# Output projection of a hybrid mixer layer: pairs of token tiles with seven block products in place of eight, conv weights split during the scan

## The chip, the cores and the metric

The kernel runs on one core of a Trainium2 chip. The metric is the device time of one execution in microseconds, as the median of several runs. One execution was also recorded by the hardware profiler; all times of single instructions come from that one. The engines are called as the profile calls them: PE (matmul), DVE (VectorE), ACT (ScalarE), POOL (GpSimd), SP (the queue from which most DMAs are issued); "PEld" is the weight load of a matmul.

## What is computed

One layer with 2176 tokens (128 of context, 2048 latent) and 1024 channels. The reference, cut to what matters:

```python
h = _rmsnorm(x, norm_g) * (1.0 + scale) + shift
proj = h @ w_in                                   # 1024 -> 4096
r, k, v, g_a, b_gate, c_gate, u_conv, g_b = split(proj)
ya, s_final = _wkv(h, token_shift(r, k, v))       # bidirectional delta-rule scan, 8 heads x 64
ya = ya * silu(g_a)                               # 512 channels ("attention half")
yb = b_gate * short_conv(c_gate * u_conv) * silu(g_b)   # 512 channels ("conv half")
u = concatenate([ya, yb], axis=-1) @ w_out        # 1024 x 1024
y = rmsnorm(x + gate * u, final_g)
```

The last two lines are what the change is about: for each of 17 tiles of 128 tokens, [ya, yb] (128 x 1024) times w_out (1024 x 1024), then a gate per channel, the residual, and a normalisation.

## The kernel before

There are three phases in one program, and a scheduler that places the instructions of each engine ahead of time: it walks the program in the order in which it is written, estimates when each instruction could run, and fixes one order for each engine from that. On the chip every engine works through its own fixed list and waits, at each instruction, for the semaphores of what it needs. So an instruction whose data come late holds up everything behind it on its engine. Only PE's list is tied to the written order during the scan, by `behind` (L834), which chains each matmul to the one ahead of it.

*Phase 1* (up to about 1006 us) makes the projections with w_in, the token shifts and the conv half yb, which is complete here and is stored to a DRAM scratch `mixT` (channels x tokens).

*Phase 2* (about 1006 to 1451 us) is the scan. It has 17 stages of two blocks; the loop over `s` in `main` (L1255) plays a string of tokens, `ROUND` (L750), for each: `S` and `b`, `B`, `L`, `u`, `U` each advance a generator of small matmuls (64 to 128 wide) and their copies, `f` and `T` finish an earlier block and store its rows of ya to `mixT`. In each round ACT copies psum to SBUF for the next step (fg<-psX, fg<-psG, E<-psE, zr, zb; L830 and L832), DVE masks and subtracts (L1042, L1049, L1110, L1148), and POOL solves the blocks' triangular systems (L948, L951), one after the other until 1322 us. Psum has eight banks: three for the states (`O.pS`), three for the small products (`O.p2`), and two more (`O.pm`) that the scan uses until stage 14 of 17 and then gives up (`O.pm.close()`).

*Phase 3* is the output projection. Float32 operands are split in a high part (fp32r) and the remainder, and a product x w is made as three matmuls, hi hi + hi lo + lo hi (`products`, L1385, L1389 to L1391). A tile of tokens is the stationary operand, four blocks of 128 channels for the conv half (CONV, rows 512 to 1023 of w_out) and four for the attention half (ATT); a matmul moves 128 x 512 of the weights. Each tile so has 2 column halves x 8 channel blocks x 3 = 48 matmuls. `weights` and `ahead` (L1395, L1401) start in the last three rounds of the scan: they load and split the four conv blocks of w_out on POOL and make the conv halves of two tiles (5 and 6), in tiles of psum called psa. `tail` (L1418) splits the attention blocks of the weights, and then, for each tile in the order TILES: loads of the mixed rows (`load_m`, L1373; mxc and mxa, cast by ACT at L1381, remainder by DVE at L1382), the residual rows (L1440), 48 matmuls in psu (24 where the conv half was made ahead), the gate product from psum on DVE (L1452; L1454 for tiles made ahead), the residual addition on POOL (L1456), squares on ACT (L1457), the scale (L1458 to L1460), the normalisation on DVE (L1462) and the store (L1463).

## Time and profile before

| | |
|---|---|
| median of 3 runs | 1641.16 us (1639.65 to 1644.22) |
| the profiled execution | 1645.99 us |
| its span, first to last instruction | 1644.2 us |
| mean granted TensorE clock | 0.976 |
| PE busy | 1517.7 us, 17160 matmuls |
| POOL busy | 589.2 us |

The profiled execution lies 4.8 us above the median, and 1.8 us of it lie outside the span. A row of a group gives the line, engine, operation, output and inputs, shapes and count; then the busy time, the mean of one instruction in ns, and the idle time of the engine ahead of these instructions with what ended most of it. A row of the timeline gives start and duration, the DMA queue or engine, line and operation, a count where rows alike were put together, and in brackets the idle time before. A row of a DMA group ends with the size of one transfer and the median time from issue to landing.

### The profile page before, as it was taken

The numbers are of one execution on the slowest core, as the hardware profiler recorded it, in microseconds if no ns is written. First come the engines' busy times: TensorE is split into PE (matmuls) and PEld (weight loads), VectorE is DVE, ScalarE is ACT, GpSimd is POOL, SyncE is SP. The second block draws the span as 40 slices with busy tenths as digits, with TensorE's granted clock in tenths as the row PEclk, the third lists the DMA queues.
The fourth block names the chain that finished last, engine by engine and source line by source line (L and its number), as shares of the span: only waits on it lengthen the run. The fifth ranks groups of instructions, "written<-read, shape, count | busy, mean of one in ns | idle before, by whom it ended". The sixth has DMA issues, their size and how long they took to land.

```text
span 1644.2 us, 42415 instructions
## 1 busy us (share of the span) xinstructions
PE 1517.7 (92%) x17160; PEld 1389.9 (85%) x17160; DVE 1100.5 (67%) x2220; ACT 764.5 (46%) x1617; POOL 589.2 (36%) x1040
## 2 busy tenths in 40 slices
PE   5899999999999999999999898988888888689998
PEld 2889998999999999999988898878777777568886
DVE  5886978784738685657788784576776764574333
ACT  4544565554425452425554023767675664432222
POOL 0011211110102021102667363888888851022221
PEclk7999999999999999999999999999999999989999
DMA  9677768664746564655867857867666754254342
GB/s 378 209 264 251 242 233 284 211 228 181 236 156 195 177 208 151 204 181 194 280 202 226 284 174 219 220 190 195 191 190 164 201 136 114 63 199 162 126 151 93
DMA packets 237988, 327.23 MB, mean 199 GB/s; under 512 B 91288, under 2 KB 191896, under 8 KB 223712
## 3 DMA queue, kind: packets, MB, share of 16 engines
q1 hardware_dynamic: 231840, 318.55, 60.8%
q0 software_dynamic: 1200, 3.93, 0.6%
q8 instruction: 135, 2.21, 0.6%
q10 hardware_dynamic: 4752, 2.04, 0.6%
q14 instruction: 61, 0.50, 0.1%
HBM read 207.92 MB, written 116.54 MB: 197 GB/s over the span
## 4 chain that ended last, share of the span: by engine, by line
PE 45%; DVE 9%; POOL 7%; ACT 5%; DMA 4%; issue 3%; SPq 0%; DVEq 0%; ACTq 0%; POOLq 0%
PE psu L1389 4%; PE psu L1390 4%; PE psu L1391 4%; PE psE L841 3%; POOL zt L951 3%; ACT fg L830 2%; POOL ztmp L948 2%; PE psS L841 2%; PE mmc L166 1%; PE mmg L168 1%; PE mmg L166 1%; PE mmg L167 1%; PE mmc L167 1%; PE mmc L168 1%; PE mmv L166 1%
## 5 line engine op out<-in xcount | busy, mean ns | idle before, releaser
L951 POOL TENSOR_TENSOR zt<-zt,ztmp 128x30 f32<-128x30 f32 (+7 forms) x390 | 153.3, 393 | 30.6
L841 PE MATMUL psE<-fg 128*64 128x128 f32 x2176 | 146.4, 277 | 3.4 <-ACT fg L830 1.8
L841 PE MATMUL psS<-sv,E 128*64 128x64 f32 x2176 | 99.4, 231 | 33.2 <-DVE sv L1148 28.5
L841 PEld LDWEIGHTS psE<-fg 128*64 128x64 f32 x2176 | 120.4, 140 | 5.0 <-ACT fg L830 2.2
L841 PEld LDWEIGHTS psS<-sv,E 128*64 128x64 f32 x2176 | 81.2, 141 | 50.7 <-DVE sv L1148 38.3
L329 POOL TENSOR_TENSOR shk<-rawl 128x384 f32<-128x384 f32 (+1 forms) x24 | 25.3, 1052 | 243.1 <-ACT rawl L325 223.8
L1049 DVE TENSOR_TENSOR fg<-psG,consts 64x256 f32<-64x256 f32 x136 | 57.4, 422 | 72.7 <-PE psG L841 35.7
L832 ACT COPY E<-psE 128x256 f32<-128x256 f32 x136 | 50.3, 372 | 107.6 <-DVE E L1110 98.5
L830 ACT ACTIVATE fg<-psX 64x512 f32<-64x512 f32 x136 | 80.4, 591 | 26.7 <-PE psX L841 24.3
L1456 POOL TENSOR_TENSOR z<-z,x 128x512 f32<-128x512 f32 x32 | 41.8, 1307 | 137.5 <-DVE z L1452 114.0
L948 POOL TENSOR_TENSOR ztmp<-ab,zt 128x60 f32<-128x60 f32 (+4 forms) x165 | 86.2, 523 | 12.9
L1110 DVE TENSOR_TENSOR E<-psE,consts 128x256 f32<-128x256 f32 x136 | 56.4, 416 | 39.1 <-PE psE L841 37.1
L329 POOL TENSOR_TENSOR shv<-rawl 128x384 f32<-128x384 f32 (+1 forms) x24 | 20.9, 870 | 166.4 <-ACT rawl L325 164.9
L1148 DVE TENSOR_TENSOR sv<-psS,pc 64x128 f32<-64x128 f32 x254 | 64.8, 277 | 22.9 <-PE psS L841 20.7
L446 POOL COPY pcs<-pp 128x6 f32<-128x6 f32 (+1 forms) x48 | 20.9, 437 | 137.8 <-ACT pp L435 133.9
L166 PE MATMUL mmc<-h,w 128*128 128x384 f32 (+1 forms) x192 | 64.7, 337 | 5.9 <-ACT q1r L327 4.1
L166 PE MATMUL mmg<-h,w 128*128 128x384 f32 (+1 forms) x192 | 64.2, 334 | 3.8 <-ACT q1v L327 3.8
L832 ACT COPY fg<-psG 64x256 f32<-64x256 f32 x136 | 49.8, 366 | 32.8 <-DMA fg<-scr_ops 17.1
L166 PE MATMUL mmb<-h,w 128*128 128x384 f32 (+1 forms) x192 | 62.9, 328 | 1.5 <-ACT ta L439 1.5
L166 PE MATMUL mmgb<-h,w 128*128 128x384 f32 (+1 forms) x192 | 64.0, 333 | 0.3 <-ACT q1r L327 0.3
L167 PE MATMUL mmg<-h,w 128*128 128x384 f32 (+1 forms) x192 | 63.9, 333 | 0.0
L166 PE MATMUL mmv<-h,w 128*128 128x384 f32 (+1 forms) x192 | 63.6, 332 | 0.2 <-ACT q1r L327 0.2
(325 smaller groups left out, 5131.3 us busy)
## 6 DMA issues: line engine op xcount, KB each, us to landing
w<-scr_wsp SPq DMA_DIRECT2D x68, 1024.0 KB, 6.6
scr_wsp<-w SPq DMA_DIRECT2D x34, 1024.0 KB, 4.9
scr_ops<-pair SPq DMA_DIRECT2D x80, 384.0 KB, 3.9
wr<-in_win SPq DMA_DIRECT2D x34, 512.0 KB, 6.3
o<-scr_ops SPq DMA_DIRECT2D x32, 512.0 KB, 4.7
fg<-scr_ops SPq DMA_DIRECT2D x120, 128.0 KB, 4.3
x<-in_x SPq DMA_DIRECT2D x17, 512.0 KB, 3.7
wadas<-in_wada SPq DMA_DIRECT2D x8, 1024.0 KB
```

The source lines that it names most:

```text
L166: T.matmul(ps[:, :n], w[:, 0, k], hh[:, 0, k, :n], start=k == 0, stop=False)
L167: T.matmul(ps[:, :n], w[:, 0, k], hh[:, 1, k, :n], start=False, stop=False)
L830: P.activation(dst, src, AF.Copy, scale=-1.0)
L832: P.copy(dst, src)
L841: r = T.matmul(*a, start=True, stop=True, **k)
L948: eng.tensor_tensor(tv, ab[:, j:j + 2, j + 2:32].unsqueeze(1).broadcast_to((128, kn, 2, n)), zt[:, :kn, j:j + 2].unsqueeze(3).broadcast_to ...
L951: last = eng.tensor_tensor(zt[:, :kn, j + 2:32], zt[:, :kn, j + 2:32], tv[:, :, r], ALU.subtract).ins
L1049: V.tensor_tensor(g.gs[H[1 - h], g.op, h, us], ps[gi][r, :, 64:128], B.mG[r, g.d].unsqueeze(1).broadcast_to((64, 4, 64)), ALU.mult)
L1148: r = V.tensor_tensor(dst, sp[gi][0:64, q], B.pc[0:64, d, 2 * p:2 * p + 2, c:c + 1].broadcast_to((64, 2, 64)), ALU.mult)
L1389: T.matmul(ps[:], mh[:, n], hi[:, cs], start=start and n == 0, stop=False)
L1390: T.matmul(ps[:], mh[:, n], lo[:, cs], start=False, stop=False)
L1391: T.matmul(ps[:], ml[:, n], hi[:, cs], start=False, stop=stop and n == 3)
```

## The change

It has three parts.

*Pairs.* Fourteen of the 17 tiles are taken two at a time (PAIRS). With tile i on top of tile j, and the conv and attention halves of the rows as the two block columns, the product with w_out is a 2 x 2 block product. In place of eight block products (each 4 channel blocks x 3 = 12 matmuls), the pair makes seven, P1 to P7, of sums: S1 = A21 + A22, S2 = S1 - A11, S3 = A11 - A21, S4 = A12 - S2 of the rows (A11 and A12 are tile i's conv and attention rows, A21 and A22 tile j's), made by POOL for each pair, and four sums of weight blocks ("forms" 0 to 3), made once. Seven additions on DVE put the products together. Each input of a product is split in hi and lo by ACT and DVE as before.

*The sums of the weights* are made in the last rounds of the scan by POOL (`sums`, four blocks of work), split, stored to a DRAM scratch `tw`, and loaded again: form 1 by `first_form` at stage 15, form 2 over the second halves of the conv weights, forms 0 and 3 in `rest`, after the scan's pools have closed.

*Earlier work.* The conv weights are split during rounds 1 to 8 (`conv_weights`, one half block of 128 x 512 per round; a raw tile with one buffer, the cast on ACT, the subtraction on DVE). Three tiles (5, 6 and 0) have their conv halves made ahead, in the scan's own banks (`fill`, token `A`), so that `O.pm` stays open to the scan's end; these matmuls are chained into PE's list (`pin`). One copy of states (`held`) goes from POOL to DVE. The rest moves tiles to places in SBUF that are free by then.

The diff, cut to its core:

```diff
-ROUND_END = "f L b L u U S b S b U S b b S L B L T S B S B S B S B B".split()
-ROUND_LAST = "S b S b S b S b".split()
+ROUND_END = "f L b L A u U S b S b U S b b S L B L A A T S B S B S B S B B".split()
+ROUND_FILL = "f L b L A u U S b S b U S b S b L B L A T S B S B S B S B".split()
+ROUND_LAST = "A S b S b S b S b A".split()
...
+        K.weights()
+        O.l1 = Pool(K, "p2l1", "left")
-        O.l1 = Pool(K, "p2l1", "left")
...
+    def pin(r):
+        behind(r, O.last)
+        O.last = r.ins
...
-                    G.tensor_copy(sv[0:64, u], held.pop(gi)[:])
+                    V.tensor_copy(sv[0:64, u], held.pop(gi)[:])
...
+            if 1 <= s <= 8:
+                next(conv)
+            if s == NST - 4:
+                fill = K.fill()
+                next(fill)
+                sums = K.sums()
+                next(sums)
+                next(sums)
             if s == NST - 3:
-                O.pm.close()
-                O.pm = None
-                K.weights()
-                tail = K.ahead()
+                K.early_att()
+                next(sums)
+                next(sums)
+            if s == NST - 2:
+                K.first_form()
...
-                run(tail)
+                run(fill)
+                O.pm.close()
+                O.pm = None
...
-    TILES = [5, 6, 7, 8, 9, 10, 11, 12, 0, 13, 14, 15, 16, 1, 2, 3, 4]
-    AHEAD = TILES[:2]
-    z0 = {}
-    def load_raw(k):
-        raw = O.r.tile([128, 1024], F32, tag="raw", name=f"woraw{k}", bufs=2)
-        D(raw[:], A["wout"][k * 128:(k + 1) * 128, :])
-        return raw
-    def load_k(k, hi, lo, eng, raw=None):
-        copy = P.copy if raw is None else G.tensor_copy
-        raw = raw or load_raw(k)
-        copy(hi[:], raw[:])
-        eng.tensor_tensor(lo[:], raw[:], hi[:].bitcast(F32), ALU.subtract)
-        wk[k] = (hi, lo)
-    def load_m(pool, i, ks, b, copy=P.copy, eng=V):
-        t0 = i * 128
-        a = "c" if ks is CONV else "a"
-        mx = O.r.tile([128, 4, 128], F32, tag="raw", name=f"mx{a}{i}", bufs=2)
-        D(mx[:], S["mixT"].rearrange("(k p) t -> p k t", p=128)[:, ks[0]:ks[0] + 4, t0:t0 + 128])
-        mh = pool.tile([128, 4, 128], F32R, tag=f"mh{a}", name=f"mh{a}{i}", bufs=b)
-        ml = pool.tile([128, 4, 128], F32R, tag=f"ml{a}", name=f"ml{a}{i}", bufs=b)
-        copy(mh[:], mx[:])
-        eng.tensor_tensor(ml[:], mx[:], mh[:].bitcast(F32), ALU.subtract)
-        return mh, ml
-    def products(ps, ms, cs, ks, start, stop):
-        mh, ml = ms
-        for n, k in enumerate(ks):
-            hi, lo = wk[k]
-            T.matmul(ps[:], mh[:, n], hi[:, cs], start=start and n == 0, stop=False)
-            T.matmul(ps[:], mh[:, n], lo[:, cs], start=False, stop=False)
-            T.matmul(ps[:], ml[:, n], hi[:, cs], start=False, stop=stop and n == 3)
+    AHEAD = [5, 6, 0]
+    PAIRS = [(7, 8), (9, 10), (11, 12), (13, 14), (15, 16), (1, 2), (3, 4)]
...
+    def split(hi, lo, raw, copy, eng):
+        copy(hi, raw)
+        eng.tensor_tensor(lo, raw, hi.bitcast(F32), ALU.subtract)
 
     def weights():
         O.r = Pool(K, "p3r", "left")
+    def conv_weights():
+        for k in CONV:
+            hi, lo = wk[k] = [O.r.tile([128, 1024], F32R, name=f"wo{x}{k}") for x in "hl"]
+            for c in HALF:
+                raw = O.r.tile([128, 512], F32, tag="raw", name=f"woraw{k}", bufs=1)
+                D(raw[:], A["wout"][k * 128:(k + 1) * 128, c])
+                split(hi[:, c], lo[:, c], raw[:], P.copy, V)
+                yield
...
+    def product(ps, m, w, start=True, stop=True, pin=lambda r: None):
+        hi, lo = m
+        for n in range(4):
+            wh, wl = w(n)
+            c = slice(n * 128, n * 128 + 128)
+            pin(T.matmul(ps[:], hi[:, c], wh, start=start and n == 0, stop=False))
+            pin(T.matmul(ps[:], hi[:, c], wl, start=False, stop=False))
+            pin(T.matmul(ps[:], lo[:, c], wh, start=False, stop=stop and n == 3))
...
+    def fill():
+        def prepare(i):
+            raw = O.r.tile([128, 512], F32, tag="raw", name=f"mxc{i}", bufs=1)
+            load_mix(raw[:], i, CONV)
+            t = K.spare(f"mhc{i}", F32R, "ab2")
+            m = t[:, 0:512], t[:, 512:1024]
+            split(*m, raw[:], G.tensor_copy, G)
+            return m
+        places = ["a1", "ztmp", "a2", "a3"]
...
+                ps = K.ps_tile([128, 512], f"psa{i}_{h}")
+                product(ps, m, plain(CONV, h), pin=K.pin)
+                if n < 2:
+                    z0[i][h] = K.spare(f"z0_{i}{h}", F32, places.pop(0), 512)[:]
+                P.copy(z0[i][h], ps[:])
+                if h and n < 2:
+                    m = prepare(AHEAD[n + 1])
...
+    def sums():
+        sub = lambda o, x, y: G.tensor_tensor(o, x, y, ALU.subtract)
+        n = 0
+        for k in range(4):
+            t = [K.spare(f"sum{x}{k}", F32, x) for x in ("o10", "o11")]
+            for x, r in zip(t, (k + 4, k)):
+                D(x[:], A["wout"][r * 128:r * 128 + 128, :])
+            (c0, c1), (a0, a1) = [[x[:, h] for h in HALF] for x in t]
+            for f, o, x, y in ((0, c0, c1, c0), (2, c1, a1, c1), (1, a1, a1, c0), (3, a0, a0, a1)):
+                sub(o, x, y)
+            for f, x in ((1, a1), (2, c1), (0, c0), (3, a0)):
+                n += 1
+                if n % 2:
+                    u = K.spare(f"sumh{n}", F32R, "ab")
+                    u = u[:, 0:512], u[:, 512:1024]
+                else:
+                    u = [K.spare(f"sumh{n}{b}", F32R, "zt", 512)[:] for b in range(2)]
+                split(*u, x, G.tensor_copy, G)
+                for b in range(2):
+                    D(S["tw"][f, b, :, k], u[b].bitcast(F32))
+            yield
...
+    def early_att():
+        att_weights(0, K.spare("woraw0", F32, "o10"), G, *[K.spare(f"wo{x}0", F32R, f"o2{n}") for n, x in enumerate("hl")])
...
+            new("A11", (i, CONV))
+            new("A21", (j, CONV))
+            new("A22", (j, ATT))
+            new("A12", (i, ATT))
+            yield f
+            for o, x, y, op in (("S3", "A11", "A21", ALU.subtract), ("S1", "A21", "A22", ALU.add), ("S2", "S1", "A11", ALU.subtract)):
+                new(o)
+                G.tensor_tensor(raw[o], raw[x], raw[y], op)
...
+            zi, zj = [[r.z[:, h] for h in HALF] for r in (ri, rj)]
+            P.copy(zi[0], made("P1", "A11", plain(CONV, 0))[:])
+            nf = next(nxt, None)
+            p2 = made("P2", "A12", plain(ATT, 0))
+            next(nxt, None)
+            p7 = made("P7", "S3", form_b(2))
+            next(nxt, None)
+            p5 = made("P5", "S1", form_b(0))
+            next(nxt, None)
+            p6 = made("P6", "S2", form_b(1))
+            add(zj[1], p6, zi[0])
+            add(zi[0], p2, zi[0])
+            half(ri, 0)
+            add(zj[0], p7, zj[1])
+            add(zi[1], p5, zj[1])
+            add(zj[1], p5, zj[0])
+            half(rj, 1)
+            next(nxt, None)
+            p4 = made("P4", "A22", form_b(3))
+            add(zj[0], p4, zj[0])
+            half(rj, 0)
+            next(nxt, None)
+            p3 = made("P3", "S4", plain(ATT, 1))
+            add(zi[1], p3, zi[1])
+            half(ri, 1)
...
+        for f in (0, 3):
+            t = [O.t.tile([128, 4, 512], F32R, name=f"t{f}{x}") for x in "hl"]
+            for b in range(2):
+                D(t[b][:].bitcast(F32), S["tw"][f, b])
+            form[f] = [[x[:, n] for n in range(4)] for x in t]
```

Line numbers below are those of the kernel that the row is from; in the changed kernel the split of weights and rows is at L1385 and L1386 with its weight loads at L1396, the matmuls at L1429 to L1431, the loads of mixed rows at L1421, the residual rows at L1539 and the loads of forms 0 and 3 at L1667.

**ACT at the scan's start.** In these rows E, fg, zr and zb are the scan's operands, psX, psG, psE and psU its psum tiles, and x2 stands for two rows alike. Before:

```order
L832 COPY E_912_11064<-psE0_1_01_11087 128x4x64
L830 ACTIVATE fg0_9816<-psX0_0_1_11196 64x2x256 x2
L830 ACTIVATE fg1_9817<-psX0_1_1_11197 64x2x256 x2
L1073 ACTIVATE zb_9826<-zc_919_11171,consts_9809 128x16x32 x2
L832 COPY fg0_9816<-psG1_0_0_11218 64x256
L832 COPY fg1_9817<-psG1_1_0_11219 64x256
```

Now (woh4 to woh7 are the high parts of the conv weights, woraw the loaded halves):

```order
L834 COPY E_912_11068<-psE0_1_01_11091 128x4x64
L1385 CAST woh4_11582<-woraw4_11584 128x512
L1385 CAST woh4_11582<-woraw4_12064 128x512
L832 ACTIVATE fg0_9817<-psX0_0_1_11200 64x2x256 x2
L832 ACTIVATE fg1_9818<-psX0_1_1_11201 64x2x256 x2
L1079 ACTIVATE zb_9827<-zc_919_11175,consts_9810 128x16x32 x2
L1385 CAST woh5_12542<-woraw5_12544 128x512
L834 COPY fg0_9817<-psG1_0_0_11222 64x256
L834 COPY fg1_9818<-psG1_1_0_11223 64x256
```

The eight casts of the conv weights, written in rounds 1 to 8, stand among the copies of the first round, the first two ahead of the first fg<-psX.

**SP at the end of the scan and the start of the projection.** Before (gb and fg are gate and gain rows, mxa and mxc a tile's attention and conv rows, x its residual rows, yo the scan's last outputs):

```order
L1424 DMA gb_18922<-scr_gate_68 128x1024 x2
L1426 DMA fg_18925<-in_fg 128x1024
L1440 DMA x35_18945<-in_x 128x1024
L1440 DMA x36_19005<-in_x 128x1024
L1186 DMA sg_1265_19137<-scr_sg_61 128x512
L1378 DMA mxa5_18939<-scr_mixT_63 128x4x128
L1220 DMA scr_mixT_63<-yo_1264_18876 128x4x128
L1378 DMA mxa6_18999<-scr_mixT_63 128x4x128
L1186 DMA w_1268_19146<-scr_q_62 128x512
L1378 DMA mxc7_19059<-scr_mixT_63 128x4x128
```

Now (rA12_7, rA11_7, rA21_7, rA22_7 are the rows of the first pair, tiles 7 and 8; t0 and t3 the forms 0 and 3; x30 and z0 belong to tile 0, x38 to tile 8):

```order
L1539 DMA x37_19388<-in_x 128x1024
L1563 DMA out_y<-z6_19191 128x1024
L1228 DMA scr_mixT_63<-yo_1276_19327 128x512
L1539 DMA x38_19392<-in_x 128x1024
L1667 DMA t0h_19340<-scr_tw_69 128x2048
L1667 DMA t0l_19341<-scr_tw_69 128x2048
L1667 DMA t3h_19344<-scr_tw_69 128x2048
L1667 DMA t3l_19345<-scr_tw_69 128x2048
L1563 DMA out_y<-z0_19250 128x1024
L1421 DMA rA11_7_19348<-scr_mixT_63 128x4x128
L1421 DMA rA21_7_19350<-scr_mixT_63 128x4x128
L1421 DMA rA22_7_19352<-scr_mixT_63 128x4x128
```

Of the first pair's rows, A12 is loaded ahead of the last blocks of the scan; the other three stand behind the 1 MB loads of the forms and the store of tile 0.

**PE at the first pair.** In the changed kernel, behind tile 0's last matmuls (psu0_1) and a last transposition of the scan (psT):

```order
L1431 MATMUL psu0_1_19269<-woh3_19096,mha0l_19243 128x512
L854 MATMUL psT1275_19322<-consts_9810,y_1175_17144 128x2x64 x4
L1429 MATMUL psP1_7_19396<-woh4_11582,A11_7h_19362 128x512
L1430 MATMUL psP1_7_19396<-wol4_11583,A11_7h_19362 128x512
L1429 MATMUL psP2_7_19418<-woh0_17873,A12_7h_19366 128x512
L1430 MATMUL psP2_7_19418<-wol0_17874,A12_7h_19366 128x512
L1431 MATMUL psP2_7_19418<-woh0_17873,A12_7l_19367 128x512
L1429 MATMUL psP2_7_19418<-woh1_19084,A12_7h_19366 128x512
L1430 MATMUL psP2_7_19418<-wol1_19085,A12_7h_19366 128x512
```

Two matmuls of P1, which read A11, stand ahead of the twelve of P2, which read A12; the rest of P1 follows behind P2.

214 lines of the change are left out of this document (152 added, 62 removed).

## The prediction

> **What bounds the kernel now.** I read the page's head first, then the table of windows over the end of the scan and the output projection, then the groups of instructions inside the projection.
>
> ```profile
> span 1644.2 us, 42415 instructions
> PE 1517.7 (92%) x17160; PEld 1389.9 (85%) x17160; DVE 1100.5 (67%) x2220; ACT 764.5 (46%) x1617; POOL 589.2 (36%) x1040
> 1350.00:1400.00 50.00, 40.44 (x708) 32.09 (x704) 21.83 (x53) 20.52 (x42) 11.09 (x17) 0.93 0.44 117
> 1400.00:1450.00 50.00, 34.33 (x731) 29.80 (x729) 28.62 (x74) 23.34 (x47) 7.09 (x3) 0.88 0.28 87
> 1450.00:1500.00 50.00, 46.41 (x207) 37.01 (x206) 30.48 (x47) 14.07 (x34) 12.00 (x9) 0.92 0.58 195
> 1500.00:1600.00 100.00, 100.00 (x432) 80.95 (x431) 39.37 (x63) 25.59 (x64) 23.31 (x18) 1.00 0.40 142
> ```
>
> The window columns are length, then busy us of PE, weight loads, DVE, ACT and POOL, then PE's granted clock, DMA share and GB/s. From 1500 to 1600 PE is never idle: 432 matmuls in 100 us, **0.2315 us** each. There the time is the number of matmuls and nothing else. The last two stretches of the scan are another matter: from 1350 to 1450 PE works 74.8 of 100 us.
>
> The projection's count comes from its tiles of psum:
>
> ```profile
> L1389 PE MATMUL psu<-woh,mha x136: 392/397/795, 1455.7 to 1635.5; 128*128 128x512 f32 x136
> L1389 PE MATMUL psu<-woh,mhc x120: 392/394/402, 1469.1 to 1632.8; 128*128 128x512 f32 x120
> L1389 PE MATMUL psa<-woh,mhc x16: 389/410/628, 1353.4 to 1379.3; 128*128 128x512 f32 x16
> 1636.17 0.25 PE psu L1391
> 1636.44 0.70 DVE z L1452
> 1639.43 0.75 DVE z L1462
> ```
>
> L1390 and L1391 have the same counts, so psu is 3 x (136 + 120) = 768 matmuls from 1455.7 to 1636.4, 0.2353 each with the slow first ones; I use 0.2325. Behind the last matmul stands a chain of 7.8 us to the end at 1644.2. The 48 psa matmuls (conv halves of two tiles) lie in the scan.
>
> **The matmuls of the projection.** A pair costs 7 x 12 = 84 matmuls instead of 96; three tiles keep their attention halves, 3 x 24 = 72. So 72 + 7 x 84 = 660 instead of 768: -108 x 0.2325 = **-25.1 us**, if PE stays the bound. What the other engines do per pair:
>
> ```profile
> L1456 POOL TENSOR_TENSOR z<-z,x 128x512 f32<-128x512 f32 x18 | 23.3, 1296 | 76.9 <-DVE z L1452 76.9
> L1452 DVE TENSOR_TENSOR z<-psu,gb 128x512 f32<-128x512 f32 x18 | 12.5, 692 | 24.8 <-PE psu L1391 24.8
> L1462 DVE SCALAR_TENSOR_TENSOR z<-z,ss,fg 128x1024 f32<-128x1024 f32 x9 | 11.6, 1285 | 0.9
> L1457 ACT ACTIVATE sq<-z 128x512 f32<-128x512 f32 x18 | 11.3, 630 | 1.6 <-POOL z L1456 1.6
> L1382 DVE TENSOR_TENSOR mla<-mxa,mha 128x512 fp32r<-128x512 f32 x9 | 6.3, 698 | 11.7 <-ACT mha L1381 11.7
> L1381 ACT CAST mha<-mxa 128x512 fp32r<-128x512 f32 x9 | 5.6, 621 | 28.1 <-DMA mxa<-scr_mixT 28.1
> ```
>
> DVE: 7 splits, 7 additions and 4 gate products at 0.69-0.70, two normalisations at 1.285, small ones 0.6: 15.7 us. POOL: 4 sums of inputs and 4 residual additions at 1.296: 10.4. ACT: 7 casts and 4 squares at 0.62-0.63, a copy and small ones: about 8.5. PE: 84 x 0.2325 = 19.5. So a pair in the middle stays at PE's pace, with 3.8 us to spare on DVE. At the end one more addition stands in the last chain: **+0.7**. The projection's first matmul is at 1455.7, and from 1450 to 1460 PE works 6.51 us of 10 (row below); in the new order six matmuls of tile 5 stand inside the last round and the rest follow weights that are split by then: **-1**, bounds -3.5 and 0.
>
> **The first pair's reload.** In SP's new order the second half of the pair's residual rows (x38), then four loads of 1 MB (t0h, t0l, t3h, t3l), then the store of tile 0's output stand ahead of rA11, rA21 and rA22 of the first pair. PE's order has two matmuls of P1, which need A11, ahead of the twelve of P2, whose input is loaded early; so nothing of the pair covers that wait.
>
> ```profile
> 1450.00:1460.00 10.00, 6.51 (x35) 5.09 (x34) 5.99 (x10) 2.69 (x5) 0.00 (x0) 0.58 0.79 268
> GB/s 378 209 264 251 242 233 284 211 228 181 236 156 195 177 208 151 204 181 194 280 202 226 284 174 219 220 190 195 191 190 164 201 136 114 63 199 162 126 151 93
> mxc<-scr_mixT SPq DMA_DIRECT2D x17, 256.0 KB, 3.2
> mxa<-scr_mixT SPq DMA_DIRECT2D x4, 256.0 KB, 7.3
> ```
>
> The last row is of the window 1440 to 1470: a 256 KB load that takes 3.2 us by the page takes 7.3 there, behind 2.5 MB of gate, gain and residual rows. Let E0 be the end of tile 0's last matmul. x38's buffer is free only after tile 0's last square: two DVE operations 1.4, POOL 1.3, square 0.63, and the first half's gate product and POOL addition ahead of them 2.0, so about E0 + 5.4; the 1 MB loads follow from E0 + 6. With x38 4.7 MB then lie ahead of rA11 (and 0.5 MB of store, issued behind tile 0's normalisation at about E0 + 8): at the page's fastest slice, 378 GB/s, 12.4 us; at the 268 GB/s of 1450 to 1460, 17.5. A11 lands at E0 + 18.4 to 23.5 and its cast ends 0.62 later. I take **+19**, near the fast end, since these are loads of long rows; bounds 0 and 24 (0 if the requests land early all the same). The wait for t0 and t3 is inside it.
>
> The Trainium skill, "DMA: Bandwidth & Descriptors", section "Queues, rings and completion order", says that completion on a queue isn't first in, first out, though each engine consumes its ring in order; by the first half of that rule rA11 could overtake, by the second hardly. The 7.3 us of the row above speak for the second. The page's "Specifications" give about 358 GB/s for one core's reads; by an estimate from it the 4.7 MB take 13.1 us and the forecast would be 1 us higher.
>
> **The conv weights in the scan's first round.** The program has eight half-pieces in rounds 1 to 8; in ACT's new order all eight casts stand in the first round, the first two ahead of the very first fg<-psX.
>
> ```profile
> 1011.51 1.20 ACT L832 COPY E<-psE 128x256 f32<-128x256 f32 x4 [7.70 <-DMA a<-scr_lo]
> 1013.96 2.41 ACT L830 ACTIVATE fg<-psX 64x512 f32<-64x512 f32 x4 [1.24 <-PE psX L841]
> 1017.62 1.67 ACT L832 COPY fg<-psG 64x256 f32<-64x256 f32 x4
> 1029.96 2.44 ACT L830 ACTIVATE fg<-psX 64x512 f32<-64x512 f32 x4 [4.04 <-PE psX L841]
> 1032.42 1.72 ACT L832 COPY fg<-psG 64x256 f32<-64x256 f32 x4
> 1135.00:1158.00 23.00, 20.16 (x568) 18.14 (x562) 15.83 (x42) 17.01 (x36) 19.98 (x44) 1.00 0.71 196
> 1017.38 0.94 SPq L890 DMA_DIRECT2D a<-scr_lo  x2
> 1018.37 1.11 SPq L988 DMA_DIRECT2D sv<-scr_vt  x2
> 1019.58 4.77 SPq L999 DMA_DIRECT2D fg<-scr_ops  x4
> sv<-scr_vt SPq DMA_DIRECT2D x3, 256.0 KB, 8.0
> woraw<-in_wout SPq DMA_DIRECT2D x8, 512.0 KB, 3.9
> ```
>
> (The row of sv is of 1014 to 1042.) SP issues the first piece behind the a loads, at 1018.4, already 4.4 us after fg<-psX had run. It lands between 3.2 (the 256 KB row) and 8.0 us (sv, issued there) later; say 6, 1024.4. Its cast 0.62 and DVE's subtraction 0.70 must end before the second load is issued, since the raw tile has one buffer: 1025.8, or behind the four fg loads; issue 0.35, landing 3.2 to 4, cast 0.62: fg<-psX starts at about 1031, 17 late. Behind fg<-psX wait psG, psU, psS and so the whole round; nothing covers it, and PE has nothing else in its order. Six more pieces at 0.35 + 3.2 to 4 + 0.62 + 0.70 = 4.9 to 5.7 us each end at 1060 to 1065; the fg<-psG copies that the last cast now stands among ran from 1032.42 to 1034.14. That would be 26 to 32 late. If every landing takes 3.2, fg<-psX comes at 1027, 13 late, and ACT's own work lies in the waits. Low end **13**, high end **33**; I take **+24**, near their middle, as later pieces run beside the delayed round's own transfers. A split has no later use that would pay it back: in a round of the middle PE works 20.16 of 23 us (88%, the row of 1135), so little can be caught up.
>
> **The end of the scan.** POOL is free from 1322.84:
>
> ```profile
> 1322.84 0.61 POOL L956 DMA_DIRECT2D scr_zt<-zt  x1 [0.30 <-POOL zt L951]
> 1354.28 1.26 POOL L1382 TENSOR_TENSOR mlc<-mxc,mhc 128x512 fp32r<-128x512 f32 x1
> L1381 POOL CAST mhc<-mxc x2: 609/610/611, 1352.7 to 1366.4; 128x512 fp32r<-128x512 f32 x2
> PE psT L848 <- DVE y L1203: 9.1, 2, 6.0
> PE psa L1389 <- POOL mhc L1381: 1.5, 1, 1.5
> ```
>
> The weight sums are four blocks of 8 subtractions at 1.26 and 4 casts at 0.61, 12.5 us a block, 50 in all: beside the scan until about 1380 to 1415 with its waits. The 24 more psa matmuls (24 x 0.2325 = 5.6) and five psum banks instead of three fall where PE idles 25 of 100 us; they can fill the 9.1 us for psT, or wait, pinned, for a cast that stands among the sums on POOL. Bounds -8 (those gaps) and +8; I take **0**. The 8 stores and 2 loads per block on SP are 40 issues at about 0.4, 16 us over four rounds, beside an SP queue idle most of that time.
>
> **The sum**, against the profiled execution (1645.99, span 1644.2): 1646.0 - 25.1 + 0.7 - 1 + 19 + 24 + 0 = 1663.6. That execution lies 4.8 above the median of the three runs, so **1659** against 1641.16.
>
> **Rivals.** R1, the splits cost nothing: it needs the first two casts to run before 1014, or ACT to take them in another order; against it speaks SP's order, in which the load follows the a loads of 1017. It gives 1659 - 24 = 1635, faster. The other side is reached from a cost of the splits under 1 us; under 11 the change is within noise. R2, the reload is hidden, since the loads land while tiles 6 and 0 run: 1640, no change; for it, the four 1 MB loads need nothing that ends late, against it, x38's buffer. R3, both: 1616. R4, both stalls and a pinned psa matmul waits for a whole block of sums: +12.5, 1671.5.
>
> **Chances.** Forecast 0.48 (its own range 1641 to 1677: -11 to +9 for the splits, -10 to +5 for the reload and 8 either way for the scan's end, not all at one end), R1 0.15, R2 0.12, R3 0.13, R4 0.12. A measurement here tells about 0.3% (4.9 us) from none. Faster: R1 and R3, 0.28. Same: most of R2, 0.10. Slower: 0.62. The range from 1617 to 1678 leaves out the far half of R3, the top of R4 and the forecast's tails, under 0.2.
>
> **What would show it.** Right: ACT idle before L1385 by several us eight times near 1020 to 1060, the first round's second fg<-psX (1029.96 before) some 20 us later; PE idle about 19 us ahead of psP1 of the first pair with the cast of A11 as releaser; 84 matmuls a pair at 0.2325. Wrong: ACT's casts without idle time ahead, psP1 directly behind psu0, DVE at 100% in the pairs, or psa waiting over 8 us.

## The result, and the profile after

The changed kernel takes **1721.66 us** (median of 4 runs, 1718.91 to 1724.74) against 1642.69 us of the kernel before (4 runs, 1639.65 to 1646.15): a ratio of 1.048, 95% interval 1.045 to 1.051. It is slower, as forecast, but by 79 us and not by 18; 1721.66 lies far outside the range that ended at 1678. The execution that was profiled took 1718.91 us (before: 1645.99).

The page's head of the changed kernel, and its windows, with the columns of those shown before (length, PE, weight loads, DVE, ACT, POOL, clock, DMA share, GB/s):

```profile
span 1717.1 us, 42574 instructions
PE 1511.3 (88%) x17076; PEld 1386.4 (81%) x17076; DVE 1184.6 (69%) x2306; ACT 783.5 (46%) x1654; POOL 670.4 (39%) x1104
1400.00:1450.00 50.00, 40.24 (x798) 34.58 (x800) 21.62 (x56) 21.24 (x45) 23.87 (x30) 0.86 0.72 218
1450.00:1500.00 50.00, 26.76 (x390) 22.13 (x386) 16.44 (x38) 13.21 (x28) 11.76 (x12) 0.75 0.49 158
1500.00:1550.00 50.00, 28.46 (x252) 21.99 (x248) 36.15 (x65) 14.28 (x32) 11.30 (x7) 0.84 0.70 251
1600.00:1700.00 100.00, 94.65 (x401) 75.92 (x400) 87.36 (x110) 33.30 (x82) 55.69 (x35) 0.98 0.40 136
```

There are 84 matmuls fewer than before (17160 to 17076: 24 more psa, 108 fewer in the projection), and PE works 6.4 us less, not the 19.5 of 84 matmuls at 0.2325; the mean granted clock is 0.952 instead of 0.976. All the added time is PE waiting: 26.76 and 28.46 busy us of 50 around the scan's end, and even in the pairs 94.65 of 100 where the projection before had 100.

The table splits the two profiled executions. The scan's rounds are cut at the first of the 128 state matmuls (psS) of each; the zero is the end of the last matmul of phase 1, since that phase varies between executions (its end lies between 1002.9 and 1010.0 us in the executions of the changed kernel and its variants). The last column sums the prediction's terms for that part.

| us | before | after | difference | predicted |
|---|---|---|---|---|
| phase 1's last matmul to the first psS | 9.6 | 23.6 | +14.0 | +24 with round 0 |
| round 0 | 25.9 | 40.4 | +14.5 | (above) |
| rounds 1 to 9 | 215.5 | 215.0 | -0.5 | 0 |
| round 10 | 25.4 | 44.1 | **+18.7** | 0 |
| rounds 11 to 14 | 120.6 | 120.4 | -0.2 | 0 |
| rounds 15 and 16 | 47.5 | 66.7 | **+19.2** | 0 |
| behind the scan's last psS | 193.4 | 204.1 | +10.7 | -6.4 |
| all behind phase 1 | 637.9 | 714.2 | +76.3 | +17.6 |

**Start and round 0.** ACT's timeline (start, duration, engine, line and operation, idle time before it), two rows of before and then those of the changed kernel:

```profile
1003.43 0.38 ACTq L807 DMA_DIRECT2D vec<-in_vec  x1
1010.01 0.47 ACTq L988 DMA_DIRECT2D sv<-scr_vt  x1
```

```profile
1010.14 0.38 ACTq L809 DMA_DIRECT2D vec<-in_vec  x1
1018.71 0.45 ACTq L994 DMA_DIRECT2D sv<-scr_vt  x1
1019.85 1.20 ACT L834 COPY E<-psE 128x256 f32<-128x256 f32 x4 [19.37 <-DMA sv<-scr_vt]
1022.26 0.62 ACT L1385 CAST woh<-woraw 128x512 fp32r<-128x512 f32 x1 [1.21 <-DMA woraw<-in_wout]
1028.26 0.62 ACT L1385 CAST woh<-woraw 128x512 fp32r<-128x512 f32 x1 [5.38 <-DMA woraw<-in_wout]
1028.90 2.41 ACT L832 ACTIVATE fg<-psX 64x512 f32<-64x512 f32 x4
1042.31 0.62 ACT L1385 CAST woh<-woraw 128x512 fp32r<-128x512 f32 x1 [2.71 <-DMA woraw<-in_wout]
1051.73 0.62 ACT L1385 CAST woh<-woraw 128x512 fp32r<-128x512 f32 x1 [3.62 <-DMA woraw<-in_wout]
```

The casts stall ACT as forecast: fg<-psX starts right behind the second one, at 1028.90 (before: 1013.96). But the E copies, ahead of any cast, already start at 1019.85 and not 1011.51: ACT's queue first issues the loads of vec and then of sv, 6.7 and 8.7 us later than before, though phase 1 ended 3.4 us earlier. Of the 28.5 us, 14.0 lie ahead of the first psS and 14.5 in round 0, where the splits are.

**Round 10.** SP's timeline, then POOL's, then a wait of DVE (total, count, longest):

```profile
1285.51 1.98 SPq L1005 DMA_DIRECT2D fg<-scr_ops  x3
1312.13 0.39 SPq L1421 DMA_DIRECT2D mxc<-scr_mixT  x1
1313.97 2.08 SPq L1034 DMA_DIRECT2D zc<-scr_zt  x2
```

```profile
1309.38 0.26 POOL L957 TENSOR_TENSOR zt<-zt,ztmp 128x30 f32<-128x30 f32 x1
1309.59 0.61 POOL L1385 CAST mhc<-mxc 128x512 fp32r<-128x512 f32 x1
1310.85 1.26 POOL L1386 TENSOR_TENSOR mhc<-mxc,mhc 128x512 fp32r<-128x512 f32 x1
```

```profile
DVE zr L1062 <- DMA zc<-scr_zt: 19.4, 1, 19.4
```

SP issues nothing from 1287.5 to 1312.1. The load at L1421 brings the next filled tile's conv rows into a raw tile with one buffer; it waits until POOL has cast and subtracted the rows in it, and POOL reaches that only behind a whole triangular solve, at 1309.59. Behind that load stand the scan's own loads of zc and fg. The code writes this load in stage 13; the scheduler placed it in round 10.

**Rounds 15 and 16.** ACT's timeline, and POOL's sums; then the windows of round 15 and of round 16, before (two rows) and after:

```profile
1454.46 0.58 ACT L834 COPY y<-psS 64x512 f32<-64x512 f32 x1 [0.26 <-DVE sv L1154]
1469.08 0.58 ACT L1460 COPY z<-psa 128x512 f32<-128x512 f32 x1 [14.04 <-DMA t_o<-scr_tw]
1364.01 1.39 POOL L1467 TENSOR_TENSOR sumo<-sumo 128x512 f32<-128x512 f32 x1 [24.18 <-DMA sumo<-in_wout]
1390.42 1.29 POOL L1467 TENSOR_TENSOR sumo<-sumo 128x512 f32<-128x512 f32 x1 [7.75 <-DMA sumo<-in_wout]
1449.44 1.27 POOL L1467 TENSOR_TENSOR sumo<-sumo 128x512 f32<-128x512 f32 x1 [10.55 <-DMA sumo<-in_wout]
1461.09 1.26 POOL L1386 TENSOR_TENSOR sumh<-sumo,sumh 128x512 fp32r<-128x512 f32 x1
1403.30:1435.10 31.80, 21.54 (x462) 18.43 (x458) 15.96 (x39) 13.26 (x29) 2.35 (x1) 0.89 0.22 66
1435.10:1450.80 15.70, 11.30 (x198) 10.20 (x196) 12.06 (x35) 6.82 (x13) 4.75 (x2) 0.81 0.48 160
1446.30:1496.00 49.70, 28.56 (x474) 24.14 (x468) 15.12 (x37) 12.64 (x26) 12.31 (x12) 0.76 0.50 161
1496.00:1513.00 17.00, 12.88 (x206) 10.84 (x204) 13.25 (x36) 8.32 (x15) 2.31 (x1) 0.90 0.42 136
```

The last block of sums starts at 1449.44 and ends at 1462.4, where 1380 to 1415 was forecast for the end: a block works some 12.5 us, as costed, but each waits for its loads and stores, and they came 26 to 32 us apart. ACT's copy of tile 0's conv half out of psa waits 14.04 us. Not all of the 19.2 us is waiting: PE is busy 8.6 us longer in these rounds, with 20 more matmuls (12 psa and 8 of tile 5's attention half) and, in round 15, a granted clock of 0.76 instead of 0.89.

**The projection.** SP's timeline and PE's waits in front of the first pair and inside the pairs, then DVE's groups between 1600 and 1700 (count, busy us, mean ns, idle before):

```profile
1540.07 0.33 SPq L1539 DMA_DIRECT2D x<-in_x  x1
1540.49 0.38 SPq L1667 DMA_DIRECT2D t0h<-scr_tw  x1
1543.13 8.04 SPq L1421 DMA_DIRECT2D rA<-scr_mixT  x3
PE psP L1429 <- ACT A_7h L1385: 25.0, 1, 25.0
PE psP L1429 <- DVE z L1623: 5.6, 4, 3.1
L1548 DVE TENSOR_TENSOR z<-z,gb 128x512 f32<-128x512 f32 x20 | 24.5, 1237 | 0.1
L1623 DVE TENSOR_TENSOR z<-psP,z 128x512 f32<-128x512 f32 x32 | 20.7, 679 | 3.8 <-DMA out_y<-z 3.3 <-PE psP L1431 0.6
L1558 DVE TENSOR_TENSOR ss<-ss 128x1 f32<-128x1 f32 x10 | 6.5, 646 | 3.8 <-ACT x L1554 3.8
```

The first pair waits as forecast, 25.0 us where 19 was taken. The additions from psum (L1623) take 679 ns, as costed; the gate product of the same size (L1548), which now has both operands in SBUF, takes 1237 ns, and the addition of two columns of 128 numbers 646 where L1458 took 160 before. From the first matmul of the pairs to the last there are 145.8 us (20.8 a pair; 19.5 forecast), with 5.6 us in which PE waits until an addition on DVE has read a psum place, and the end chain is 13.8 us (7.8 before).

### The profile page after: what moved, and what is told of

It is laid out like the page before. It is cut to its first block, busy times and chain, and to the rows that moved or that the text cites. A ratio compares the mean times of both kernels' runs of the same rounds, so it can differ in the third digit from the quotient of the medians.

```text
span 1717.1 us, 42574 instructions
## 1 busy us (share of the span) xinstructions
PE 1511.3 (88%) x17076; PEld 1386.4 (81%) x17076; DVE 1184.6 (69%) x2306; ACT 783.5 (46%) x1654; POOL 670.4 (39%) x1104
## 5 line engine op out<-in xcount | busy, mean ns | idle before, releaser
L843 PE MATMUL psE<-fg 128*64 128x128 f32 x2176 | 152.2, 285 | 12.1 <-ACT fg L832 6.9
L843 PEld LDWEIGHTS psE<-fg 128*64 128x64 f32 x2176 | 125.5, 145 | 13.7 <-ACT fg L832 7.8
L832 ACT ACTIVATE fg<-psX 64x512 f32<-64x512 f32 x136 | 80.4, 592 | 16.3 <-PE psX L843 13.8
L1116 DVE TENSOR_TENSOR E<-psE,consts 128x256 f32<-128x256 f32 x136 | 56.5, 416 | 42.2 <-PE psE L843 41.1
L329 POOL TENSOR_TENSOR shv<-rawl 128x384 f32<-128x384 f32 (+1 forms) x24 | 20.8, 865 | 162.7 <-ACT rawl L325 162.5
L446 POOL COPY pcs<-pp 128x6 f32<-128x6 f32 (+1 forms) x48 | 20.8, 434 | 138.9 <-ACT pp L435 138.6
L843 PE MATMUL psG<-fg,o 64*64 64x128 f32 x1088 | 45.0, 280 | 28.9 <-ACT E L834 24.6
L166 PE MATMUL mmc<-h,w 128*128 128x384 f32 (+1 forms) x192 | 64.6, 336 | 5.9 <-ACT q1r L327 4.1
L166 PE MATMUL mmg<-h,w 128*128 128x384 f32 (+1 forms) x192 | 63.7, 332 | 3.8 <-ACT q1v L327 3.8
L834 ACT COPY fg<-psG 64x256 f32<-64x256 f32 x136 | 49.8, 366 | 35.0 <-DMA fg<-scr_ops 17.1
L843 PEld LDWEIGHTS psG<-fg,o 64*64 64x64 f32 x1088 | 35.9, 136 | 35.6 <-ACT E L834 29.0
L167 PE MATMUL mmc<-h,w 128*128 128x384 f32 (+1 forms) x192 | 63.7, 332 | 0.0
```

The costliest lines, as they stand in the source:

```text
L166: T.matmul(ps[:, :n], w[:, 0, k], hh[:, 0, k, :n], start=k == 0, stop=False)
L167: T.matmul(ps[:, :n], w[:, 0, k], hh[:, 1, k, :n], start=False, stop=False)
L329: G.tensor_tensor(s[:, lo:n].rearrange("p (r c) -> p r c", c=64), rp[:, :R, 0:64], rp[:, :R, 2:66], ALU.add)
L446: G.tensor_copy(pcs[:, d, c0 - pc0:c0 - pc0 + nch], pt[:, :nch, 64 - 64 * d])
L832: P.activation(dst, src, AF.Copy, scale=-1.0)
L834: P.copy(dst, src)
```

## The experiments

Each is one execution with a profile; the kernel before ran beside them at 1640.69 to 1648.92 us. "Behind phase 1" is the last row of the table above (after: 714.2, before: 637.9). Parts that an experiment doesn't touch scatter: round 0 from 38.7 to 41.1, rounds 1 to 9 from 212.5 to 215.4, round 10 from 44.1 to 49.0, rounds 11 to 14 from 116.4 to 123.5, rounds 15 and 16 from 62.8 to 66.7. The diffs are cut to their core. In them `K.hold(r)` chains an instruction behind the last scan matmul written so far, so that the scheduler can't place it earlier, and `K.after(r, x)` chains it behind the instruction x.

**1. The splits, held in their rounds.**

```diff
+                K.hold(D(raw[:], A["wout"][k * 128:(k + 1) * 128, c]))
+                yield
+                K.hold(P.copy(hi[:, c], raw[:]))
```

> The conv splits are tied to their written rounds: each load behind the last scan matmul issued when its round begins, each cast behind that of the next round. Theory (the waits are in series and the one in stage 10 ends at a time of its own): the first round falls from 40.4 to about 26 us, stage 1 starts near 1052, but the stall of stage 10 ends when POOL leaves the solve at about 1312 whatever the scan does, so it grows from 20 to about 34 us and stage 11 still starts near 1326; total 1715 to 1722. Rival (each wait is worth its own length): total about 1704.

1709.16 us; behind phase 1 701.7. Round 0 falls from 40.4 to 21.5, below that of before; rounds 1 to 9 pay 4.7 of it back (219.7). The splits' stall is real and worth about 19 us in its round, 12.5 net. Round 10 takes 46.5, within its scatter, so it did not grow by what round 0 gave back: these two waits are not in series. The late start (24.0) is untouched, so it isn't theirs.

**2. The rows of the filled tiles, held in stage 13.**

```diff
-            load_mix(raw[:], i, CONV)
+            K.hold(load_mix(raw[:], i, CONV))
```

> The loads of the conv rows of tiles 5, 6 and 0 are tied to a scan matmul of the round in which they are written (stage 13 on). Theory: SP no longer waits in stage 10 for POOL, that round falls from 44 to 24 to 26 us, and the time falls by 17 to 20 us to 1699 to 1702. Rival (POOL's solves are what the scan waits for there): the wait stays with another name, total 1713 to 1720.

1707.58 us; behind phase 1 695.8. Round 10 falls from 44.1 to 23.0, and DVE's wait for zc is gone; rounds 11 to 14 take 126.2 (120.4). The gain behind phase 1 is 18.4 us, as expected; the time itself fell less, since phase 1 ended 7.1 us later in this execution. The load on SP's queue is shown as the cause of round 10.

**3. The sums ahead of the early attention weights.**

```diff
-                K.early_att()
                 next(sums)
                 next(sums)
+                K.early_att()
```

> The split of attention block 0, which uses the sums' buffer o10, moves behind the last two blocks of sums. Theory: the sums end about 12 us earlier, their last store lands before the copy of tile 0's psum needs the place, and the round of stage 15 falls from 50 to 36 to 39 us; total 1705 to 1709. Rival: the first copy of tile 0 is late because the sums as a chain are late (loads and stores behind each other on SP), and stays so: total 1715 to 1720.

1730.50 us; behind phase 1 718.7, rounds 15 and 16 69.7. No gain, and slower than either account allowed: the sums end 12.8 us into round 15 instead of 16.0, ACT's copy still waits, 14.2 us, and round 10, which the edit doesn't touch, takes 49.0.

**4. The first pair's rows ahead of the forms and of its residual rows.**

```diff
-                D(t[b][:].bitcast(F32), S["tw"][f, b])
+                    K.after(D(tt[f][b][:].bitcast(F32), S["tw"][f, b]), after)
...
+            if i in PAIRS[0]:
+                K.after(q, lastld[0].ins)
```

> The first pair's rows are loaded ahead of the four 1 MB forms, and its residual rows behind them. Theory: P1 starts 3.2 us of landing and 0.6 of cast behind the issue, some 12 to 15 us earlier than now; forms 0 arrive before P5 needs them, 36 matmuls later; total 1704 to 1708. Rival (the forms are the bound, P5 waits for them as long as P1 did): total 1713 to 1720.

1714.96 us; behind phase 1 707.1, of which the part behind the scan 195.5 (204.1). PE's wait before psP falls from 25.0 to 10.1. So the order on SP's queue made most of that wait. The time lies where the rival put it, but not for its reason: PE doesn't wait for the forms. It waits 9.5 us for DVE's additions in the pairs (5.6 before), and the pairs take 152.7 us instead of 145.8.

**5. The last block of sums doesn't use the place of tile 0's half.** The half of tile 0 that ACT copies shares a place ("ab") with the odd split sums. The last block's go elsewhere:

```diff
-                if n % 2:
+                if n % 2 and k < 3:
```

> The last block of sums puts its split halves in the two zt places alone, so the place ab, into which ACT copies tile 0's first conv half, is free once the third block is stored. Theory: ACT's copy no longer waits 11 to 14 us, the rounds of stages 15 and 16 together fall from 67 to 52 to 56 us, and from the last dense matmul to the end 714 falls to 700 to 704. Rival: the copy then waits for the third block's stores nearly as long, or another wait follows: 710 to 718.

1725.16 us; behind phase 1 715.1, no gain. The copy's 14 us are gone (0.6 are left), and these stand in their place:

```profile
DVE yo L1222 <- DMA scr_mixT<-yo: 16.5, 1, 16.5
PE psS L843 <- DVE so L1154: 16.8, 3, 15.8
POOL sumh L1386 <- DMA scr_tw<-sumh: 7.7, 4, 3.8
```

The scan's store of yo stands on SP's queue behind the stores and reloads of the sums, and these wait for POOL. One wait covered another. The forecast's rival had this.

**6. Another DVE instruction for products and subtractions.**

```diff
-        eng.tensor_tensor(lo, raw, hi.bitcast(F32), ALU.subtract)
+            V.scalar_tensor_tensor(lo, raw, 1.0, hi.bitcast(F32), ALU.mult, ALU.subtract)
```

> In the projection DVE's subtractions of the splits and its gate products are written as scalar_tensor_tensor with a factor of 1.0, the values unchanged. Theory (DVE's tensor_tensor on two SBUF operands doesn't start while POOL runs, and scalar_tensor_tensor does): the gate product falls from 1.24 us to 0.65 to 0.75 us on average, the seven pairs take 137 to 141 us of PE instead of 146, the last chain shortens by 0 to 2; from the last dense matmul to the end 714 falls to 704 to 709. Rival (any DVE instruction waits for POOL): mean 1.2 us as before and 712 to 716.

1720.79 us; behind phase 1 714.5, no change. Between 1600 and 1660 us the gate product's mean is 1447 ns (1452 with the instruction of before). The theory that this other instruction avoids the wait falls.

**7. The scan's first loads from SP.**

```diff
     def setup_rest():
-        D = P.dma_start
+        D = nc.sync.dma_start
```

> The three small loads at the scan's start (vec, pc) go from ACT's queue to SP's. Theory (ACT's copies of E, and with them the scan, stand behind these loads, whose issue waits for earlier transfers): the first psS comes 14 to 17 us after the last dense matmul instead of 23.6, and the end 5 to 9 us earlier, if the stall of stage 10 does not take it back; with it taken back the first round starts earlier and stage 11 does not. Rival: the sv loads behind them wait as long, 22 to 24.

1723.33 us; behind phase 1 715.1. The start falls from 23.6 to 17.0, but ACT then waits 12.25 us for woraw in round 0, which takes 48.6. So 6.6 of the 14.0 us of the start are shown to be the place of the loads of vec and pc; alone it brings nothing, since the splits behind it take the time. The loads of sv stay on ACT's queue here, and the other 7.4 us were not separated.

**8. All of these together** (1, 2, 4, 5, 6, 7).

> All the edits that took a wait away together: conv splits in their rounds, conv rows of three tiles held until stage 13, the last sums off the place ab, first pair's rows ahead of the forms, scalar_tensor_tensor in the projection, small loads on SP. Theory (the waits add up): first round 21 to 23 us, stage 10 23 to 25, stages 11 to 14 120 to 126, stages 15 and 16 52 to 56, tail 183 to 189; from the last dense matmul 630 to 648, total 1633 to 1655. Rival (waits replace each other): over 670.

1674.45 us; behind phase 1 666.7: 47.5 of the 76.3 us are gone, where 630 to 648 was expected if all waits added up. Alone, experiments 1, 2 and 4 brought 12.5, 18.4 and 7.1 and the other three nothing, so some edits pay only beside others. Start 17.8, round 0 22.7, round 10 24.4. Rounds 15 and 16 stay at 61.9, with DVE's wait for the store of yo (15.9), and behind the scan it takes 195.3, because the pairs got slower: 154.5 us from the first matmul to the last, with 11.1 us in which PE waits for DVE's additions.

**9. The sums' loads and stores on POOL's queue**, beside the edits of 8. Two things more are changed: the reloads of forms 1 and 2 are held behind the scan's matmuls, and form 1's reload starts one stage later.

```diff
-                    D(S["tw"][f, b, :, k], u[b].bitcast(F32))
+                    G.dma_start(S["tw"][f, b, :, k], u[b].bitcast(F32))
```

> Edits: those of e7_all, and the sums' own transfers (reloads of the transposed weights and stores of the sums) are issued by POOL's queue in place of SP's. Theory (in stages 15 and 16 the scan's stores and loads stand on SP's queue behind the sums' stores and reloads, which wait for POOL): DVE's wait of some 16 us on the store of yo goes, stages 15 and 16 together fall from 61.9 to 47 to 52 us, and the time after the last dense matmul from 666.7 to 652 to 657 us. Rival (some 40 transfers issued at about 0.6 us each on POOL delay the solves or the sums by as much, or the wait moves on to the forms): stages 15 and 16 stay at 58 us or more, and the time after the last dense matmul at 664 us or more.

1669.04 us; behind phase 1 662.1, rounds 15 and 16 55.8: between the two. No wait of DVE for the store of yo is left. In kernel 8 SP issues that store at 1444.30, behind eight stores of sums and eleven reloads of forms that it issues between 1420 and 1442, so the queue held it; which of the three changes freed it isn't separated, and only 6 us come of it. Of the 8.3 us to the 47.5 of before, 5.1 are more work of PE in these rounds (37.90 busy us against 32.84).

**10. The pairs with half of POOL's work**, beside the edits of 8 (not 9). The residual rows are left out of all pairs but the last.

```diff
+            if r.i in AHEAD or r.last:
                 (V if r.last else G).tensor_tensor(z[:, c], z[:, c], r.x[:, c], ALU.add)
```

> Edits: those of e7_all, and POOL's addition of the residual to the output is left out for all pairs but the last, so the output lacks the residual there. Theory (in the pairs DVE's operations with two operands in SBUF do not start while POOL works, and DVE is the bound): with half of POOL's work in the pairs gone, the stretch from the first to the last matmul of the output projection falls from 154.5 us in e7_all to 137 to 142 us, and DVE's subtraction for the hi and lo halves from a mean of about 1240 ns to under 1000 ns. Rival (DVE's own work or other waits bound the pairs, and the longer subtraction only fills idle time): 150 us or more, whatever the mean of the subtraction.

1652.87 us; the matmuls of the pairs take 141.7 us (20.2 a pair) instead of 154.5. A window of 100 us in the pairs, of kernel 8 and of this one, then the gate product of kernel 8 and two groups of DVE of this one:

```profile
1540.00:1640.00 100.00, 88.94 (x364) 71.16 (x363) 91.01 (x110) 34.66 (x82) 58.51 (x36) 0.93 0.45 147
1530.00:1630.00 100.00, 97.15 (x420) 78.33 (x419) 80.75 (x125) 38.38 (x92) 31.08 (x20) 1.00 0.50 168
L1556 DVE SCALAR_TENSOR_TENSOR z<-z,gb 128x512 f32<-128x512 f32 x16 | 21.3, 1341 | 0.1
L1556 DVE SCALAR_TENSOR_TENSOR z<-z,gb 128x512 f32<-128x512 f32 x20 | 15.1, 777 | 0.1
L1638 DVE TENSOR_TENSOR z<-psP,z 128x512 f32<-128x512 f32 x35 | 22.6, 681 | 13.0 <-DMA out_y<-z 13.0
```

With POOL at 31.08 instead of 58.51 us, DVE's gate product goes from 1341 to 777 ns, though nothing of DVE's own work was touched, and PE is busy again: its waits for DVE's additions fall from 11.1 to 2.8 us. The subtractions of the splits fall less, from 1017 to 887 ns on average. POOL's work beside DVE's was what held the pairs of kernel 8; that the removed addition also stood between the gate product and ACT's square is not separated from it.

**11. The same cost in the kernel before.** There PE is the bound, and POOL has little to do. POOL gets two, three or four more additions per half tile (four shown):

```diff
+                if not last:
+                    for _ in range(4):
+                        G.tensor_tensor(xt[:, cs], xt[:, cs], xt[:, cs], ALU.add)
```

> The kernel before, with two more additions on POOL behind each residual addition of the projection (they double the residual rows in place, which nothing reads any more; nothing else is changed). Theory (DVE's operations with all operands in SBUF and POOL's operations take turns, so their times add up, while DVE's operations with an operand in PSUM go beside POOL's): per tile POOL now works 6 x 1.296 = 7.8 us, DVE's SBUF operations 2 x 0.69 + 1.285 + 0.16 = 2.8, together 10.6 us under PE's 11.15, so the time stays within 8 us of the kernel before; but the splits and normalisations that meet POOL get longer: the splits' mean rises from 0.69-0.70 to over 0.9 us and the normalisation's from 1.285 to over 1.5, while the gate product from PSUM stays within 0.03 of 0.692. Rival (POOL and DVE do not hold each other up, and the longer operations in the changed kernel have another cause): the means stay within 0.1 us of those before.

> The kernel before, with three more additions on POOL behind each residual addition of the projection (as in the run with two). Theory: per tile POOL 8 x 1.296 = 10.4 us and DVE's SBUF operations 2.8, in turns 13.2 us against PE's 11.15, so each of some 15 tiles gets about 2 us longer: the stretch of the projection's matmuls grows from 180.7 to 200 to 215 us, and the time by 20 to 35. Rival (POOL and DVE work side by side): POOL's 10.4 us stay under PE's 11.15, the stretch stays under 188 us.

Two: 1642.65 us (before beside it 1642.88); three: 1643.63. Groups of DVE, and POOL's added one, from 1500 to 1630 with two:

```profile
L1452 DVE TENSOR_TENSOR z<-psu,gb 128x512 f32<-128x512 f32 x24 | 16.5, 689 | 12.4 <-PE psu L1391 12.3
L1465 DVE SCALAR_TENSOR_TENSOR z<-z,ss,fg 128x1024 f32<-128x1024 f32 x12 | 16.0, 1330 | 1.2
L1382 DVE TENSOR_TENSOR mlc<-mxc,mhc 128x512 fp32r<-128x512 f32 x11 | 15.2, 1383 | 17.6 <-ACT mhc L1381 17.6
L1459 POOL TENSOR_TENSOR x<-x 128x512 f32<-128x512 f32 x47 | 56.3, 1197 | 3.7
```

The splits of the conv rows, with two SBUF operands, double (692 to 1383), the product from psum stays (689), and the normalisation rises less than expected: 10 of 12 found POOL idle, the other two took 1.55 us. With three the time was to grow by 20 to 35 us and didn't: the added operation reads the same rows twice and takes 1.03 us alone, not 1.296, so the sum was 8.8 + 2.8 us a tile, hardly above PE's 11.15. So four:

> The kernel before, with four more additions on POOL behind each residual addition of the projection. The run with three showed that such an addition (both inputs the same rows) takes 1.03 us and not 1.296, so that its sum was not above PE's pace. Now per tile POOL works 2 x 1.29 + 8 x 1.03 = 10.8 us, under PE's 11.15, and DVE's SBUF operations 2.8. Theory (the two take turns): 13.6 us a tile, some 0.4 less for records that overlap by 0.04 us each, so about 2 us more for each of some 15 tiles: the stretch of the projection's matmuls grows from 182 to 202 to 218 us, and the time by 20 to 36. Rival (they only lengthen each other's records, and what is lost is found again): the stretch stays under 188 us.

1675.75 us (before beside it 1640.69): +35. That lies in the range expected, but not by the way expected. The matmuls still end after 184.2 us, where 202 to 218 was forecast and under 188 by the rival: PE has six psum places of half a tile each and can run three tiles ahead, so the delay shows behind its last matmul, 33.1 us instead of 7.8. The normalisations tell the pace (first and last start; the first row, of the kernel before, is the semaphore event of L1462, with the same first and last start as its operations):

```profile
L1462 DVEq EVENT_SEMAPHORE  x16: 21/21/21, 1470.9 to 1628.9; - x16
L1465 DVE SCALAR_TENSOR_TENSOR z<-z,ss,fg x16: 1427/1433/2055, 1474.9 to 1656.3; 128x1024 f32<-128x1024 f32 x16
```

15 steps in 158.0 us before and in 181.4 with the load, 23 us more, although POOL's own 10.8 us a tile were under PE's pace. A step takes 12.1 us, where DVE and POOL in strict turns would need 13.6. The other 12 us weren't split up; among them DVE waits 7.1 us for the last tile's residual rows, which come late, since the added operations hold their buffers.

## Why the prediction was right or wrong

- **Right: slower, and by stalls that eat the saved matmuls.** The matmuls fell by the counted number.
- **The splits in the first round: right in place and mechanism, the size in part luck.** +24 was forecast for start and round 0, +28.5 measured; but 14.0 of it is the later start, which the prediction didn't cost and which stays when the splits are held (experiment 1). There ACT's queue issues loads ahead of the first E copy, while the prediction only looked at the casts. The splits alone are worth about 19 us in round 0 and 12.5 net. (The late casts' 26 to 32 us come to 26 to 31 by its own figures; nothing hangs on it.)
- **The reload: right, undersized.** 25.0 us for 19. The forms, x38 and the store lie ahead as described; experiment 4 takes 15 us of the wait away. The load of x38 is issued 8.1 us behind tile 0's last matmul, where 5.4 was taken, and A11's cast starts 16.7 us after that; from 1540 to 1557 the DMA engines moved 348 GB/s, between the 378 and the 268 of the two bounds. With it and the three smaller points here, the part behind the scan is +17.1 off: reload 6.5 (25.5 us from tile 0's last matmul to the first of the pairs), pairs 9.1, end chain 5.3, and -3.8 in the rest.
- **Wrong, and the largest: the step "The end of the scan".** It put 0 for the filled tiles and the sums, with bounds of 8 us, and called SP's queue "idle most of that time". It counted issue times (16 us) but not what an issue waits for. A load whose buffer POOL still reads, and stores of sums that POOL has not made, hold everything behind them on SP. Round 10 (+18.7) is shown to be this by experiment 2. For rounds 15 and 16 (+19.2) the waits for stores and reloads of sums are in the trace, but no experiment took more than 11 us of them away, and 8.6 are more work of PE. The two are 38 of the 59 us that the forecast of the profiled execution missed behind phase 1. The load was in SP's new order, ahead of zc; the prediction looked at that order only at the start and at the end. For rounds 15 and 16 rival R4 named a pinned psa matmul that waits for a block of sums, and gave it 12.5 us; the wait was of that size (11.2 on PE, over the 8 us that the prediction named as a sign of being wrong), but came from ACT's copy and, behind that, from SP. Nor did the sums start when POOL's solves were over: the first began at 1364.01, after POOL had waited 24.18 us for the load of its weight rows.
- **Wrong: the step "a pair in the middle stays at PE's pace, with 3.8 us to spare on DVE".** It added up DVE (15.7) and POOL (10.4) side by side. They don't run side by side: 87.36 busy us in 100 are 18.2 a pair of 20.8. The pairs took 9 us more than forecast in the changed kernel, 5.6 of them PE's waits for DVE, and more (154.5 - 7 x 19.5 = 18) once the other waits were gone. With half of POOL's work they take 141.7, 5 over the forecast (experiment 10).
- **What is left open.** The slower rounds 1 to 9 of experiment 1, the rest of rounds 15 and 16, and why the start stays at 17 in kernels 7 to 10. None of the kernels with a complete output beats the one before; the best (1669.04) is 20 us slower than the 1648.92 beside it. Kernel 10, which is kernel 8 without most residual additions, comes to 1652.87, 0.24% above the same 1648.92, one execution against one: even then the saved matmuls only just pay for the sums, the splits and the additions around them.

## What to carry to other kernels

When work is moved beside a full pipeline, look at every queue between its old and its new place, and ask of each transfer that is added what it waits for, not how long its issue takes: one load with a single buffer behind a busy engine stops all that is issued after it. Fewer matmuls are worth their time only if the engines around them have room; add POOL's time to DVE's where DVE reads both operands from SBUF. When a wait is removed, expect the next one under it: experiments 3, 5, 6 and 7 each brought nothing alone, 1, 2 and 4 brought 38.0 us one by one, and six edits together brought 47.5.

## What the hardware showed

DVE and POOL take turns where DVE's operation has two operands in SBUF. In the records of the pairs such an operation that starts while POOL works ends 0.55 us after POOL's operation, nearly whatever its start. Of L1548 and L1386, 39 started while POOL worked (beside two in the last 0.06 us of a POOL operation); five had begun within 0.01 us of POOL's operation and went first, and the other 34 all ended 0.546 to 0.557 us behind POOL's. POOL's operation waits too: 1.29 us alone, mostly 1.6 to 1.84 when it meets one of these. The timelines of DVE and of POOL in one such stretch:

```profile
1628.21 3.48 DVE L1548 TENSOR_TENSOR z<-z,gb 128x512 f32<-128x512 f32 x2
1631.61 1.78 DVE L1386 TENSOR_TENSOR S<-rS,S 128x512 fp32r<-128x512 f32 x1
1629.41 5.14 POOL L1553 TENSOR_TENSOR z<-z,x 128x512 f32<-128x512 f32 x3
```

Three operations that take 0.68 us alone fill 5.18 us on DVE, and three of 1.29 fill 5.14 on POOL. With one operand in psum (L1623) the mean is 0.677 us when POOL works and 0.681 when it doesn't, and the reciprocal takes 0.162 with three additions on POOL (L1463) and 0.164 without them (L1460). The kernel before shows the same at the edge: one split that began 0.25 us ahead of the end of POOL's addition took 0.80 us, again 0.547 beyond it; two that began 0.22 and 0.18 ahead took 0.76 and 0.73, and the others began at most 0.15 us before POOL was done or later, so its 0.69 said nothing of this cost.

The Trainium skill, "SBUF — State Buffer", section "Who interferes with whom", says that a DVE instruction with two SBUF inputs contends with a GpSimd instruction that reads SBUF, and that one with at most one SBUF input does not, outside the modes in which DVE uses two ports. The trace agrees on both sides (1237 ns against 679 in the changed kernel). The Trainium skill, "SBUF — State Buffer", section "SBUF: two separate sides", says that whoever starts first gets the shared ports for the whole instruction. Here a DVE operation of 0.68 us made POOL's 0.45 us longer, so the records overlap by some 0.2 us.

In experiment 11 POOL's addition of a tile to itself took 1.03 us alone, where that of two different tiles took 1.29.
